# Input weights split once, kept in device memory as two parts, and read back by the later blocks

## The chip, the cores and the metric

The kernel runs on one core of a Trainium2 chip. The metric is device time in microseconds of one execution. A core has TensorE (PE, with its weight loads as PEld), VectorE (DVE), ScalarE (ACT), GpSimd (POOL) and SyncE (SP), each working through a queue of its own in order, and 16 DMA engines, to which here nearly every transfer is issued from SP's queue.

## The reference

One encoder layer over two sequences, of 1024 and 2048 tokens with 1024 features, in float32. A normed residual goes through one input projection. Its columns feed an FNet group (zf, uf) and a bidirectional Mamba-2 group (z, x, B, C, dt), and the two outputs go through an output projection and a gated embedding.

```python
u = rms_norm(h, norm_w)
proj = u @ w_in                     # 1024 -> 2*512 + 1536 + 2560 + 48
z_f, u_f, z_s, xbc, dt_raw = jnp.split(proj, [...], axis=-1)
y_f = einsum(real(fft2(u_f)), w_fmix) * silu(z_f)
xbc = silu(conv1d(xbc, width 5) + conv_b)
xs, Bm, Cm = jnp.split(xbc, [D_SSM, D_SSM + N_BC_GROUPS * D_STATE], axis=-1)
dt_f, dt_b = softplus(dt_raw + bias)
y_s = ssd(xs, dt_f, A_f, Bm, Cm) + flip(ssd(flip(xs), flip(dt_b), ...)) + D * xs
y_s = group_rms_norm(y_s * silu(z_s)) * ssd_norm_w
h = h + concat([y_f, y_s]) @ w_out
h = h + (p @ w_ple_in) * sigmoid(h @ w_ple_gate)
return rms_norm(h, final_norm_w)
```

## The kernel before, in words

The work has two phases. The first, to about 1970 us, is the input projection with the convolution and the state-space scan. It goes over three blocks of 1024 tokens: the short sequence, and the two halves of the long one (with two tokens of overlap). The second phase is the Fourier transform, the output projection and the gated embedding; nothing in it is edited.

In a block, the normed tokens stand transposed in SBUF in three parts of 342 columns, each as a high part uh, rounded to the type in which TensorE reads it, and a low part ul, the remainder. A block has 40 jobs, one per 128 columns of w_in (4 C, 4 B, 12 x, 12 z, 4 uf, 4 zf), and one short job dt. A job's weights are treated as the tokens are: a load brings 128 columns of w_in into wr (512 KB in pieces of 512 bytes), ACT casts it to wh, and POOL subtracts to get wl. wr has one buffer, wh and wl two each. A job has three pieces, one per token part: 24 matmuls into a PSUM bank (wh with uh, wh with ul, wl with uh, for each of eight row groups), and one eviction by ACT. All three blocks load and split the same weights.

The order of all of this is written by hand, in slots. Each piece of a job is a slot; `pre(s, f)` puts f ahead of the piece of slot s in the queues of the engines that it uses, `post(s, f)` behind it. A list `rows_` sets the order of the jobs: the first row interleaves C, dt and B piece by piece, then come uf0 and, for each of 12 units (two heads of the scan), x, z and one other job; the last row interleaves uf3 and zf3. Nine slots make a unit's cycle. A unit's `plan` places its steps by slot: loads of the broadcast rows R (rows_in, 256 KB a piece) and er (decays), POOL's cut of R (rows_cut), ACT's exponentials, DVE's joins, PE's diag, POOL's weighting xw (weighted) for PE's states, the products across, POOL's gating of y with z (in the second block with two more multiplications, L662 and L663) and the stores of y.

`split_at` and `load` of a job are set by the loop over `coming`: a job is split in the slot after the last piece of the job two before it, three slots ahead of its own first piece, and its load is issued one slot behind the split of the job before, which is five slots ahead. The load then waits, on SP, until POOL has read wr for that job.

At a block's start the dt job's result is transposed (dt_turned), goes through a long chain on DVE (dt_softplus, to atm), and is summed by PE (dt_sums, tile pcs, copied by ACT to acs) and transposed again (dt_rows, tile prw), stored, and read back as R and er. In a block's last row, x_in loads the next block's token tiles, x_norm scales them on DVE and x_turn transposes them on PE (tile pt) into uh and ul.

Of the kernel before, what the change touches and what calls it, by code (L numbers as in the profile page):

```python
# [56 lines left out]
def tile_hybrid_encoder(ctx: ExitStack, tc: tile.TileContext, a):  # L57
# [20 lines left out]
    WSd = [dram.tile([P, 7, 4, 512], F32, name=f"WSd{i}") for i in range(3)]  # L78
    PLd = dram.tile([P, 2, DM], F32, name="PLd")
# [22 lines left out]
    with ExitStack() as ph:  # L102
# [76 lines left out]
        def weights_in(c0):  # L179

            raw = wp.tile([P, KT, P], F32, tag="wr", bufs=1, name="wr")
            nc.sync.dma_start(raw, w_in[:, c0:c0 + P].rearrange("(k p) c -> p k c", p=P))
            return raw

        def weights_split(raw):

            wh = wp.tile([P, KT, P], F32R, tag="wh", name="wh")
            wl = wp.tile([P, KT, P], F32R, tag="wl", name="wl")
            S.copy(wh, raw)  # L189
            G.tensor_tensor(wl, raw, wh.bitcast(F32), op=ALU.subtract)  # L190
            return wh, wl

# [43 lines left out]
        U = {}  # L236

# [74 lines left out]
        class Job:  # L312
# [8 lines left out]
            def load(self):  # L321
                self.raw = weights_in(self.c0)

            def split(self):
                self.w = weights_split(self.raw)
# [404 lines left out]
        for bi, B in enumerate(blocks):  # L730
# [3 lines left out]
            rows_.append((B, [J("dt"), J("C"), J("B")] if bi else [J("C"), J("dt"), J("B")], "first"))  # L734
# [10 lines left out]

        n_, coming = 0, []
        for _, js, _ in rows_:
            for k, j in enumerate(js):
                j.last = n_ + 2 * len(js) + k
                if j.c0 is not None:  # L750
                    coming.append(j)
            n_ += 3 * len(js)
        coming[0].split_at = coming[1].split_at = -1
# [21 lines left out]
        with tc.manual_schedule():  # L775
# [23 lines left out]
            for i in range(3, 9):  # L799
                if i > 3:  # L800
                    pre(i - 4, x_norm, b0, i)
                if i > 5:
                    pre(i - 6, x_in, b0, i)
                post(i - 3, x_turn, b0, i)
            pre(9, decay_rates)
            for B, js, what in rows_:
# [24 lines left out]
                for si in range(3):  # L831
                    for j in js:
                        step(lambda: j.piece(si))
# [552 lines left out]
```

## Time and profile before

| | us |
|---|---|
| median of 3 runs | 3038.52 (3036.92 to 3041.12) |
| the profiled execution, whole | 3031.59 |
| its span, first to last instruction | 3029.8 |
| PE busy | 2836.0 (94%) |
| DVE / POOL / ACT busy | 2228.9 / 1475.5 / 1389.1 |
| DMA: share of the 16 engines on SP's queue | 60.6%, 436.50 MB |
| mean granted TensorE clock | 0.972 |

Busy times overlap; only what PE waits for, or what slows its clock, can change the span. Lines are those of the kernel before; an arrow to the left stands between the tile written and those read, or between an instruction and what ended its wait.

### The profile page before, as it was taken

The page shows a single profiled execution, that of the slowest core. Times are in us where ns is not written, and L with a number is a line of the kernel's source. Part 1 is how long each engine was busy: PE and PEld are TensorE (multiplying, and loading weights), DVE is VectorE, ACT ScalarE, POOL GpSimd, SP SyncE. Part 2 cuts the span into 40 slices and gives each one's busy share as a digit, 9 for nine tenths or more (in the row PEclk, how much of TensorE's full clock was granted, in tenths as well). Part 3 has the DMA queues.
Part 4 walks back from the last instruction along what each step waited for, and adds up shares of the span by engine and source line. Part 5 has one row for each costly group of instructions (what it writes and reads, how often), then busy time and mean ns, then how long its engine had stood idle before and what let it go on. Part 6 is the DMA issues. An engine that isn't in the chain of part 4 may idle for free. (4 is left out here: it accounts for less than half of the span.)

```text
span 3029.8 us, 47051 instructions
## 1 busy us (share of the span) xinstructions
PE 2836.0 (94%) x17252; PEld 2566.2 (85%) x17252; DVE 2228.9 (74%) x3412; ACT 1389.1 (46%) x2980; POOL 1475.5 (49%) x1114
## 2 busy tenths in 40 slices
PE   6899999989999899989999999969999899989998
PEld 6899989988999889989999999957677677768887
DVE  3687767666687568666779787687989988875665
ACT  4444545434544454434544444434433533354554
POOL 1355645431567565642555655455777578610000
PEclk9999999999999999999999999979999999999999
DMA  3378878972588778862677787566554644352221
GB/s 96 76 129 162 158 157 173 139 142 79 125 171 167 152 181 165 154 167 64 127 154 146 159 144 158 117 210 250 173 184 132 236 149 150 133 198 91 94 85 69
DMA packets 454579, 440.56 MB, mean 145 GB/s; under 512 B 24384, under 2 KB 405444, under 8 KB 450508
## 3 DMA queue, kind: packets, MB, share of 16 engines
q1 hardware_dynamic: 454060, 436.50, 60.6%
q8 instruction: 137, 2.24, 0.3%
q14 instruction: 94, 0.77, 0.1%
q10 hardware_dynamic: 288, 1.05, 0.1%
HBM read 328.41 MB, written 110.10 MB: 145 GB/s over the span
## 5 line engine op out<-in xcount | busy, mean ns | idle before, releaser
L361 PE MATMUL ps<-uh,wh 128*128 128x342 f32 (+1 forms) x2880 | 961.6, 334 | 8.4 <-ACT uh L267 8.4
L361 PE MATMUL ps<-ul,wh 128*128 128x342 f32 (+1 forms) x2880 | 926.3, 322 | 2.5 <-DVE ul L268 2.5
L361 PE MATMUL ps<-uh,wl 128*128 128x342 f32 (+1 forms) x2880 | 927.4, 322 | 0.4 <-POOL wl L190 0.4
L190 POOL TENSOR_TENSOR wl<-wr,wh 128x1024 fp32r<-128x1024 f32 x120 | 305.5, 2546 | 707.9 <-ACT wh L189 650.5
L361 PEld LDWEIGHTS ps<-uh,wh 128*128 128x128 f32 x2880 | 552.2, 192 | 20.1 <-ACT uh L267 9.2
L361 PEld LDWEIGHTS ps<-ul,wh 128*128 128x128 f32 x2880 | 554.5, 193 | 4.2 <-DVE ul L268 3.5
L361 PEld LDWEIGHTS ps<-uh,wl 128*128 128x128 f32 x2880 | 550.4, 191 | 1.2 <-POOL wl L190 1.1
L558 ACT ACTIVATE R<-R,lb 128x128 f32<-128x128 f32 x1152 | 356.8, 391 | 98.3 <-POOL R L548 98.2
L548 POOL TENSOR_SCALAR_AFFINE_SELECT R<-R 128x512 f32<-128x512 f32 x288 | 257.5, 905 | 193.7 <-DMA R<-ROWd 187.2
L618 DVE SCALAR_TENSOR_TENSOR H<-H,cd,pst 128x64 f32<-128x64 f32 x888 | 182.6, 274 | 47.7 <-PE pst L607 44.6
L402 DVE SCALAR_TENSOR_TENSOR xT<-raw,cvt,xT 128x1024 f32<-128x1024 f32 x144 | 214.8, 1492 | 2.6
L1102 PE MATMUL X<-whP,ah 128*128 128x512 f32 x480 | 195.2, 407 | 8.0 <-ACT pu L1111 6.4
L1102 PE MATMUL X<-wlP,ah 128*128 128x512 f32 x480 | 193.6, 403 | 1.6 <-DVE wlP L861 1.6
L1102 PE MATMUL X<-whP,al 128*128 128x512 f32 x480 | 192.5, 401 | 2.4 <-DVE al L1073 2.4
L587 POOL TENSOR_TENSOR xw<-xm,wd 128x512 f32<-128x512 f32 x144 | 181.8, 1268 | 18.7 <-PE pst L607 18.5
L367 ACT COPY raw<-ps 128x342 f32<-128x342 f32 x180 | 78.3, 438 | 241.7 <-PE ps L361 226.8
L1214 POOL TENSOR_TENSOR ht<-ht,pu 128x512 f32<-128x512 f32 x96 | 151.9, 1590 | 63.1 <-ACT pu L1111 43.0
L607 PE MATMUL pst<-xw,Bm 128*128 128x128 f32 x1056 | 151.3, 285 | 24.0 <-POOL xw L587 23.8
L607 PEld LDWEIGHTS pst<-xw,Bm 128*128 128x128 f32 x1056 | 131.9, 192 | 41.6 <-POOL xw L587 30.3
L189 ACT CAST wh<-wr 128x1024 fp32r<-128x1024 f32 x120 | 125.8, 1049 | 67.9 <-DMA wr<-in_w_in 67.2
L1073 DVE TENSOR_TENSOR al<-s,ah 128x512 fp32r<-128x512 f32 x144 | 143.6, 1021 | 16.4 <-ACT ah L1072 16.3
L563 DVE TENSOR_TENSOR R<-R,R 128x512 f32<-128x512 f32 x144 | 134.1, 931 | 25.9 <-ACT R L558 23.5
(264 smaller groups left out, 5703.9 us busy)
## 6 DMA issues: line engine op xcount, KB each, us to landing
R<-ROWd SPq DMA_DIRECT2D x288, 256.0 KB
wr<-in_w_in SPq DMA_DIRECT2D x120, 512.0 KB
er<-EXPd SPq DMA_DIRECT2D x288, 128.0 KB
Hd<-ht SPq DMA_DIRECT2D x48, 512.0 KB
ht<-Hd SPq DMA_DIRECT2D x48, 512.0 KB
y<-Yd SPq DMA_DIRECT2D x46, 512.0 KB
wlP<-WSd SPq DMA_DIRECT2D x21, 1024.0 KB
Yd<-y SPq DMA_DIRECT2D x72, 256.0 KB
```

The lines of the kernel that those rows point to most:

```text
L190: G.tensor_tensor(wl, raw, wh.bitcast(F32), op=ALU.subtract)
L361: T.matmul(ps[:, :n], lhsT=wt[:, kt, :], rhs=ut[:, kt, :n], start=(i == 0), stop=(i == 3 * KT - 1))
L402: V.scalar_tensor_tensor(dst, raw[:, k:k + TB], cvt[:, 20 * k + ct:20 * k + ct + 1], dst, op0=ALU.mult, op1=ALU.add)
L548: G.affine_select(out=R.rearrange("p c h l -> p (c h) l"), in_=R.rearrange("p c h l -> p (c h) l"), pattern=[[0, 4], [sgn, P]], compare_op ...
L558: S.activation(R[:, c, h, :], R[:, c, h, :], AF.Exp, bias=self.B.lb[:, 2 * p + c, hc + h:hc + h + 1])
L563: V.tensor_tensor(E[0], E[0], E[1], op=ALU.add)
L587: G.tensor_tensor(xw, self.xm[c4].rearrange("p c (h e) -> p c h e", h=2), col(self.B.wd[:, c4:c4 + 4, hc:hc + 2]).broadcast_to([P, 4, 2, 6 ...
L607: T.matmul(pst[:, c, :], lhsT=B.Bm[self.g][:, c4 + c, :], rhs=xw[:, c, :, :].rearrange("p h e -> p (h e)"), start=True, stop=True)
L618: V.scalar_tensor_tensor(dst[:, e], H[d][:, cc, e], B.cd[:, cc, hc + h:hc + h + 1], pst[:, c, e], op0=ALU.mult, op1=ALU.add)
L1073: V.tensor_tensor(al, src, ah.bitcast(F32), op=ALU.subtract)
L1102: T.matmul(ps, lhsT=at[:, k, :], rhs=wt[:, k, :], start=(first and i == 0), stop=(i == 11), skip_group_check=not first)
L1214: return lambda t: G.tensor_tensor(h, h, t, op=ALU.add)
```

## The change

The first block splits each job's weights as before, and two slots behind the split it stores wh and wl to device memory (WPd, 512 KB each, in rows of 4 KB). The second and third blocks load both parts into wh and wl and round them in place with two ACT copies; they have no subtraction on POOL. In all blocks a job's load now stands in the slot after the last piece of the job two before (three slots ahead of its first piece), and the split or rounding one slot ahead of the first piece. B has a row of its own behind the first one; the last row's pieces take another order; the steps of dt and of the next block's tokens have other slots.

```diff
+    WPd = [[dram.tile([P, KT, P], F32, name=f"WPd{i}_{x}") for x in range(2)] for i in range(C_DT // P)]
...
             def load(self):
-                self.raw = weights_in(self.c0)
+                if self.B.bi == 0:
+                    self.raw = wp.tile([P, KT, P], F32, tag="wr", bufs=1, name="wr")
+                    nc.sync.dma_start(self.raw, w_in[:, self.c0:self.c0 + P].rearrange("(k p) c -> p k c", p=P))
+                else:
+                    self.w = self.places()
+                    for x, wt in enumerate(self.w):
+                        nc.sync.dma_start(flat(wt).bitcast(F32), flat(WPd[self.c0 // P][x]))
+
+            def places(self):
+                return [wp.tile([P, KT, P], F32R, tag=f"w{x}", name=f"w{x}") for x in "hl"]
 
             def split(self):
-                self.w = weights_split(self.raw)
+                if self.B.bi == 0:
+                    self.w = wh, wl = self.places()
+                    S.copy(wh, self.raw)
+                    G.tensor_tensor(wl, self.raw, wh.bitcast(F32), op=ALU.subtract)
+                    for x, wt in enumerate(self.w):
+                        pre(slot[0] + 2, nc.sync.dma_start, flat(WPd[self.c0 // P][x]), flat(wt).bitcast(F32))
+                else:
+                    for wt in self.w:
+                        S.copy(flat(wt), flat(wt).bitcast(F32))
...
-                    conv(16 + i, self.dst, CT, s_ + (2 if i else 4))
+                    conv(16 + i, self.dst, CT, s_ + (2 if i else 3))
...
-            rows_.append((B, [J("dt"), J("C"), J("B")] if bi else [J("C"), J("dt"), J("B")], "first"))
+            rows_.append((B, [J("dt"), J("C")] if bi else [J("C"), J("dt")], "first"))
+            rows_.append((B, [J("B")], None))
...
+                turn = [(0, 0), (0, 1), (1, 0), (0, 2), (1, 1), (1, 2)]
...
-            j, k = coming[m], coming[m - 1]
-            j.split_at = max(coming[m - 2].last + 1, k.split_at + 2)
-            pre(k.split_at + 1, j.load)
-            pre(j.split_at, j.split)
+            j = coming[m]
+            j.load_at = coming[m - 2].last + 1
+            pre(j.load_at, j.load)
+            pre(max(j.first - 1, j.load_at), j.split)
...
-            for i in range(3, 9):
+            for i, (n_in, n_norm, n_turn) in enumerate(
+                    ((0, 0, 0), (0, 0, 0), (0, 0, 1), (0, 1, 2), (1, 2, 2), (1, 2, 3)), 3):
...
-                    post(q + 7, dt_turned, B)
-                    pre(q + 8, dt_softplus, B, 0)
-                    pre(q + 9, dt_softplus, B, 1)
-                    post(s0 + 13, dt_sums, B)
-                    post(s0 + 14, dt_rows, B)
-                    pre(s0 + 16, dt_out, B)
+                    post(q + 5, dt_turned, B)
+                    pre(q + 6, dt_softplus, B, 0)
+                    pre(q + 7, dt_softplus, B, 1)
+                    post(q + 10, dt_sums, B)
+                    post(q + 12, dt_rows, B)
+                    pre(q + 14, dt_out, B)
...
-                    for i, s_ in enumerate((2, 3, 4, 4, 5, 6, 8, 9, 10)):
-                        pre(s0 + (0, 0, 1, 2, 2, 3, 5, 6, 7)[i], x_in, b, i)
+                    for i, s_ in enumerate((3, 4, 5, 5, 6, 7, 7, 8, 9)):
+                        pre(s0 + (0, 0, 1, 2, 3, 4, 5, 6, 7)[i], x_in, b, i)
```

What this moves is seen best in three queues. The first is SP's in the middle of the first block, through some five slots of a unit's cycle: wr is a weight load, er and R are the broadcast rows, Yd and WPd stores. Before:

```order
L182 DMA wr<-in_w_in 128x8x128
L667 DMA Yd_60<-y 128x512
L540 DMA R_3261<-ROWd_67 128x2x256
L540 DMA R_3263<-ROWd_67 128x2x256
L635 DMA er_3318<-EXPd_70 64x4x128 x2
L635 DMA er_3321<-EXPd_70 64x4x128 x2
L182 DMA wr<-in_w_in 128x8x128
L635 DMA er_3434<-EXPd_70 64x4x128 x2
L635 DMA er_3437<-EXPd_70 64x4x128 x2
```

And with the change:

```order
L315 DMA wr<-in_w_in 128x8x128
L192 DMA wb<-in_w_out 128x2x256 x2
L676 DMA Yd_60<-y 128x512
L549 DMA R_3371<-ROWd_67 128x2x256
L549 DMA R_3373<-ROWd_67 128x2x256
L278 DMA WPd_0_130<-wh 128x1024
L278 DMA WPd_1_131<-wl 128x1024
L644 DMA er_3434<-EXPd_70 64x4x128 x2
L644 DMA er_3437<-EXPd_70 64x4x128 x2
L315 DMA wr<-in_w_in 128x8x128
```

Two stores per job now stand ahead of the er loads and of the next weight load, which holds its place behind the first four er loads.

The second is the same queue at the same place of the third block. Before:

```order
L182 DMA wr<-in_w_in 128x8x128
L667 DMA Yd_62<-y 128x512
L540 DMA R_17481<-ROWd_69 128x2x256
L540 DMA R_17483<-ROWd_69 128x2x256
L288 DMA UFd_64<-ft 128x1024
L635 DMA er_17544<-EXPd_72 64x4x128 x2
L635 DMA er_17547<-EXPd_72 64x4x128 x2
L182 DMA wr<-in_w_in 128x8x128
```

With the change:

```order
L319 DMA wh<-WPd_0_108 128x1024
L319 DMA wl<-WPd_1_109 128x1024
L192 DMA wb<-in_w_ple_gate 128x2x256 x2
L676 DMA Yd_62<-y 128x512
L549 DMA R_17637<-ROWd_69 128x2x256
L549 DMA R_17639<-ROWd_69 128x2x256
L278 DMA UFd_64<-ft 128x1024
L644 DMA er_17702<-EXPd_72 64x4x128 x2
L644 DMA er_17705<-EXPd_72 64x4x128 x2
L319 DMA wh<-WPd_0_158 128x1024
L319 DMA wl<-WPd_1_159 128x1024
```

Each weight load has become two, at the same point between the other transfers, but for a job that is due two slots sooner; and where it waited for POOL's reading of wr it now waits for PE's last piece of the job two before.

The third is ACT's at the start of the second block, around the copy of the sums, acs (ft and raw are evictions of pieces, CT and BT the convolutions' tiles, rows the transposed sums). Before:

```order
L406 ACTIVATE CT<-raw,cvt 128x1024
L406 ACTIVATE BT<-raw,cvt 128x1024
L371 COPY ft<-ps 128x342
L371 COPY ft<-ps 128x340
L189 CAST wh<-wr 128x1024
L367 COPY raw<-ps 128x342
L410 ACTIVATE raw<-CT 128x1024
L410 ACTIVATE raw<-BT 128x1024
L367 COPY raw<-ps 128x342
L471 COPY acs<-pcs 128x512
```

With the change:

```order
L334 CAST wh<-wh 128x1024
L334 CAST wl<-wl 128x1024
L376 COPY raw<-ps 128x342
L380 COPY ft<-ps 128x342
L419 ACTIVATE raw<-CT 128x1024
L415 ACTIVATE BT<-raw,cvt 128x1024
L380 COPY ft<-ps 128x342
L480 COPY acs<-pcs 128x512
```

The copy of the sums stood behind the tanh of both C and B, and now stands behind that of C alone.

More of the change, by code (lines that the diff above doesn't have):

```diff
@@ L177, in dt_weights @@
             V.tensor_tensor(wdt[:, :, 1, :], wdr, wdt[:, :, 0, :].bitcast(F32), op=ALU.subtract)
[L179 to L191, printed above, removed]
         def weight_sums(i, s0):
@@ L236, in tile_hybrid_encoder, with flat @@
         U = {}
+        def flat(t):
+            return t.rearrange("p k c -> p (k c)")
         def x_normed(b, i, xn):
@@ L743, in tile_hybrid_encoder @@
             rows_.append((B, [J("uf", 3), J("zf", 3)], "last"))
-        n_, coming = 0, []
[L747 to L753, printed above, removed]
+        pieces = []
+        for B, js, what in rows_:
+            if what == "last":
+                turn = [(0, 0), (0, 1), (1, 0), (0, 2), (1, 1), (1, 2)]
+            else:
+                turn = [(k, si) for si in range(3) for k in range(len(js))]
+            pieces.append([(js[k], si) for k, si in turn])
+        n_, coming = 0, []
+        for row in pieces:
+            for j, si in row:
+                if si == 0:
+                    j.first = n_
+                    if j.c0 is not None:
+                        coming.append(j)
+                j.last = n_
+                n_ += 1
         for m in range(2, len(coming)):
-            j, k = coming[m], coming[m - 1]
-            j.split_at = max(coming[m - 2].last + 1, k.split_at + 2)
-            pre(k.split_at + 1, j.load)
-            pre(j.split_at, j.split)
+            j = coming[m]
+            j.load_at = coming[m - 2].last + 1
+            pre(j.load_at, j.load)
+            pre(max(j.first - 1, j.load_at), j.split)
         xs = {}
@@ L830, in tile_hybrid_encoder @@
                             pre(s0 + 2 * i, norm_piece, BLOCKS[bi + 1], i)
-                for si in range(3):
-                    for j in js:
-                        step(lambda: j.piece(si))
+                for j, si in row:
+                    step(lambda: j.piece(si))
             while before or behind_:
```

12 lines of the change are left out of this document (6 added, 6 removed).

## The prediction

> **What bounds the kernel now.** I read the profile by stretches first: the three blocks' long middle parts (from a block's first z job to the start of its last row of jobs) and the two borders between them. The columns are microseconds, then busy time of each engine with its count, the granted TensorE clock, the share of the 16 DMA engines, and GB/s.
>
> ```profile
> 107.90:631.50 523.60, 511.70 (x3580) 493.16 (x3579) 375.26 (x649) 264.21 (x604) 276.61 (x218) 0.99 0.80 147
> 631.50:751.30 119.80, 105.41 (x695) 100.46 (x694) 81.72 (x116) 42.39 (x90) 32.52 (x22) 0.93 0.48 110
> 751.30:1300.50 549.20, 519.87 (x3603) 499.16 (x3601) 389.53 (x669) 266.24 (x605) 332.08 (x258) 0.98 0.77 157
> 1300.50:1420.00 119.50, 105.75 (x697) 100.69 (x696) 81.83 (x118) 42.47 (x90) 44.32 (x30) 0.93 0.44 119
> 1420.00:1937.60 517.60, 512.91 (x3624) 495.12 (x3622) 395.16 (x674) 246.10 (x570) 275.43 (x218) 1.00 0.71 143
> ```
>
> The three middle parts do nearly the same matmuls (3580 to 3624). The third block has PE busy 512.9 of 517.6 us at full clock: nothing can be won there. The first is 6 us longer, the second 31.6 us longer. The two borders run at clock 0.93 with 14 us of idle PE each. So PE bounds the kernel, and the change, which leaves every matmul in place, can only win what these stretches lose: some 32 us in the second block, the borders, and the start.
>
> The waits of PE (and then of the split) say what the second block loses. The first two rows are the second block's middle part alone: total wait, number, longest. The last two are groups of the page: busy time and mean ns, then idle time before and what ended it.
>
> ```profile
> PE pst L607 <- POOL xw L587: 17.4, 11, 3.8
> PE pd L575 <- ACT wh L189: 6.2, 1, 6.2
> ...
> L190 POOL TENSOR_TENSOR wl<-wr,wh 128x1024 fp32r<-128x1024 f32 x120 | 305.5, 2546 | 707.9 <-ACT wh L189 650.5
> L189 ACT CAST wh<-wr 128x1024 fp32r<-128x1024 f32 x120 | 125.8, 1049 | 67.9 <-DMA wr<-in_w_in 67.2
> ```
>
> POOL makes the low part wl in 2.55 us, 120 times, and its queue stands 650.5 us behind ACT's cast for it. The weighted inputs xw, for which PE waits, are next in that queue.
>
> **The change, part by part.** *POOL and ACT in blocks two and three.* 80 subtractions of 2.55 us (204 us) leave POOL; ACT gets 80 more copies of 1.05 us (84 us). ACT is busy 246 of 517.6 us in the third block, so 42 us more there lie beside PE; only their lateness can cost (below). In the second block the xw waits (17.4 us, plus half clock behind the longer ones) lose their cause in the queue. POOL keeps three multiplications per half unit there, and the pd wait (6.2 us) stems from ACT standing before a load, which the change keeps. I take 20 of the 31.6 us; bounds 0 (POOL late by its own work) and 32.
>
> *The dt chain.* It moves two pieces earlier, and between sums and rows stand two pieces instead of one. Start, duration, instruction; in brackets the idle time and its releaser:
>
> ```profile
> 716.76 0.86 DVE L433 TENSOR_TENSOR pv<-ptd,pv 128x256 f32<-128x256 f32 x2 [8.78 <-ACT pv L432]
> 726.27 4.23 DVE L461 SCALAR_TENSOR_TENSOR dtm<-dtm,dz 128x512 f32<-128x512 f32 x3
> 730.54 2.87 DVE L441 SCALAR_TENSOR_TENSOR dtm<-dtm,dz 128x512 f32<-128x512 f32 x4
> 733.44 0.69 DVE L442 SCALAR_TENSOR_TENSOR dtm<-dtm,de 128x512 f32<-128x512 f32 x1
> 734.17 2.77 DVE L443 SCALAR_TENSOR_TENSOR dtm<-dtm,dmx 128x512 f32<-128x512 f32 x1
> 736.98 0.69 DVE L446 TENSOR_TENSOR atm<-dtm,arep 128x512 f32<-128x512 f32 x1
> 737.59 2.60 DVE L402 SCALAR_TENSOR_TENSOR CT<-raw,cvt,CT 128x1024 f32<-128x1024 f32 x2
> ...
> 725.93 2.57 POOL L190 TENSOR_TENSOR wl<-wr,wh 128x1024 fp32r<-128x1024 f32 x1 [5.29 <-ACT wh L189]
> 733.56 2.83 POOL L190 TENSOR_TENSOR wl<-wr,wh 128x1024 fp32r<-128x1024 f32 x1 [5.06 <-ACT wh L189]
> ...
> 724.46 0.45 ACT L371 COPY ft<-ps 128x342 f32<-128x342 f32 x1 [3.47 <-PE ps L361]
> 731.98 0.44 ACT L371 COPY ft<-ps 128x340 f32<-128x340 f32 x1 [3.31 <-PE ps L361]
> 745.31 1.06 ACT L410 ACTIVATE raw<-CT 128x1024 f32<-128x1024 f32 x1 [9.14 <-DVE CT L402]
> 749.12 0.59 ACT L471 COPY acs<-pcs 128x512 f32<-128x512 f32 x1
> ...
> 749.76 1.91 PE L493 MATMUL prw<-ident,acs 128*64 128x128 f32 x8 [4.81 <-ACT acs L471]
> ```
>
> ACT stood 9.1 us before the C tanh, acs came behind it, and PE waited 4.81 us. Now: the DVE chain from pv (716.8) to atm (737.7) takes 20.9 us, of which L461 and L443 lose about 2.1 us each (three at 0.72 are 2.15, not 4.23; 0.69, not 2.77) exactly while POOL runs wl. Without wl it is 16.7 us. Two evictions 7.52 us apart two pieces on give 3.76 us a piece, so the sums stand five pieces (18.8 us) behind the turned dt, and the rows seven (26.3 us). Only the C taps (two of 2.60) then lie ahead of acs, with tanh and the small copies some 8.5 us: 25.2 us, just in time. In the first block wl stays; I leave 3 us there. The wait and its half clock:
>
> ```profile
> 745.00:750.00 5.00, 0.24 (x2) 0.21 (x3) 4.93 (x6) 3.23 (x5) 0.00 (x0) 0.84 0.00 0
> 750.00:755.00 5.00, 5.00 (x21) 4.76 (x20) 2.56 (x5) 4.21 (x7) 0.00 (x0) 0.50 0.01 2
> ...
> PE prw L493 <- ACT acs L471: 17.2, 3, 7.6
> ```
>
> At clocks 0.84 and 0.50 the two stretches lose 3.3 us beside the wait. Three waits of 17.2 us and 9.9 us of clock are 27.1; I take -24 (bounds -27 and -10, if DVE is as late as now).
>
> *The borders.* Each first x tile gets one more piece between its load and its transposes, the last three one less. PE's waits for these transposes, first border and then second:
>
> ```profile
> PE pt L264 <- DVE H L618: 5.0, 2, 3.5
> PE pt L264 <- DVE xt L250: 4.4, 1, 4.4
> ...
> PE pt L264 <- DVE H L618: 6.3, 2, 3.3
> PE pt L264 <- DVE xt L250: 2.2, 1, 2.2
> ```
>
> These are 17.9 us; clock 0.93 over 119.8 us loses 8.4 a border, less the 3.3 of acs, so 10.2 for both: 28 in all. One piece is about the longest wait (4.4), but the three late tiles have less room: -18 (bounds -28 and 0).
>
> *The start.* The second and third parts of the first block are wanted one and two pieces earlier. PE already waits there:
>
> ```profile
> PE ps L361 <- ACT uh L267: 8.4, 3, 6.4
> ```
>
> A piece less of cover is about 4 us; some of it comes back at its loads, which are also earlier: +5 (bounds 0 and +12).
>
> *The stores.* In the first block SP issues two stores of 512 KB per job behind the row loads, and the loads R, er and wr queue behind their bytes. The trace has no such store; the price comes from a late stretch whose DMAs are 512 KB pieces:
>
> ```profile
> 2850.00:2925.00 75.00, 75.00 (x355) 61.16 (x354) 50.36 (x81) 41.93 (x81) 0.00 (x0) 1.00 0.23 81
> ...
> 160.00:175.00 15.00, 15.00 (x108) 14.61 (x107) 14.00 (x22) 6.23 (x14) 7.04 (x4) 1.00 1.00 119
> 190.00:205.00 15.00, 15.00 (x108) 14.24 (x107) 14.86 (x27) 8.72 (x22) 8.28 (x7) 1.00 0.59 106
> ```
>
> 0.23 of 75 us moved 6.1 MB, so 1.05 MB take 3.0 us of all engines. A job lasts 15.2 us (517.6 us for the 34 jobs of the third middle part), so 34.4 jobs add 103 us to 0.80 of 523.6 us (419): 522, a share of 1.00. Stretches of 15 us do reach 1.00 while PE runs without a gap, others have 0.59, so the room is there, but all of it is used. If it fits, the cost is 0; if the engines hold no more than 0.90 over the block, the part lasts 580 us, +56. I take +25, nearer to fitting since PE bore 1.00 for single stretches. In blocks two and three the loads double, at 0.77 and 0.71 of the engines, so the share stays below the first block's.
>
> *Weights later.* Until now loads were issued five pieces before use and split three before; now the load stands three pieces ahead, the rounding one. In the later blocks it also waits until PE has done with the buffers, so it has 15.2 us. Issue and cast behind it, second block and third:
>
> ```profile
> 893.28 0.38 SPq L182 DMA_DIRECT2D wr<-in_w_in  x1
> 907.01 1.05 ACT L189 CAST wh<-wr 128x1024 fp32r<-128x1024 f32 x1 [4.56 <-DMA wr<-in_w_in]
> ...
> 1602.37 0.38 SPq L182 DMA_DIRECT2D wr<-in_w_in  x1
> 1613.27 1.05 ACT L189 CAST wh<-wr 128x1024 fp32r<-128x1024 f32 x1
> ...
> 1153.56 0.66 PE L575 MATMUL pd<-R,xm 128*64 128x128 f32 x8 [2.48 <-ACT R L558]
> 1154.00:1158.00 4.00, 4.00 (x20) 3.85 (x16) 3.96 (x10) 1.58 (x6) 0.00 (x0) 0.58 0.90 193
> ```
>
> At most 10.9 us to land in the third block; with half of the 3.0 us for the second part and two casts of 1.05 that is 14.5 of 15.2: just in time. In the second 13.7 + 3.6 is 17.3: 2.1 us late, for the one load in three that follows the er loads, some 11 times: 23 us there, and half clock behind the longer ones, as behind the 2.48 us wait (clock 0.58 in the next 4 us). ACT, blocked in front of these casts, delays evictions and R's exponentials too. POOL's relief lets SP run earlier: +10 (bounds 0 and +45).
>
> By the Trainium skill (TensorE: Matmul & The Clock Gate, § Why this matters for your kernels) only idle gaps over about 3 us drop the clock, so late weights of 2 us would cost no clock. This trace shows half clock after 2.48 us, so it does not bear the rule out at that length. By the rule this term would be some 5 us lower, and the sum with it.
>
> Sum: -20 - 24 - 18 + 5 + 25 + 10 = -22 against the profiled execution's 3031.6 us (span 3029.8): 3009.6. The median of the runs, 3038.5, is 6.9 above it: 3016.
>
> **The rivals.** *B, the stores fill the DMA queue: slower.* The place is the first block's middle part, the price above. Without the stores the sum is -47, so it decides above +53, where the DMA engines stay under 522/577 = 0.90. At 0.90 the time is 3048, at 0.85 (614 us, +90) 3081. For it: 1.00 needed on average where 0.80 was held, and one queue on which the loads PE depends on follow the stores. Against it: PE loses little today with 1.00 in single stretches.
>
> *C, all cover holds.* Stores and weights cost nothing, the second block becomes the third (-32), borders and acs go whole (-28, -27), start +4: -83, 2956. For it: DVE, too, gains 2.1 us wherever wl stood beside an operation as at 726 and 734, up to 80 times in blocks two and three. Against it: the loads' 13.7 us. The Trainium skill (SBUF — State Buffer, § Who interferes with whom) has DVE instructions with two SBUF inputs block on GpSimd ones that read SBUF; the two rows agree.
>
> *D, no change.* PE takes the same waits under other names: xw's become those for R's loads or for wh, and the stores eat the borders. 3038. For it: waits of PE in block two end on ACT behind a load as well.
>
> **How the numbers follow.** The forecast A has 0.44 (2995 to 3032), B 0.28, C 0.12, D 0.16. A measurement of this kernel tells 0.2%, 6 us, from no change. Faster holds A and C, 0.56; same D, 0.16; slower B, 0.28. The range cuts the outer third or so of B and most of C: 2975 to 3072.
>
> **What would show it.** Right: no PE wait for acs in blocks two and three, second middle part near 530 us, xw waits under 5 us, wl's group at 40 in POOL, first middle part near 550 us with a DMA share over 0.95. Wrong: PE waits ending on casts of wh and wl, repeated each third job; a first part over 575 us; x-tile waits still at the borders; half clock spread through blocks two and three.

## The result, and the profile after

The changed kernel takes 3134.94 us (median; 3133.49 to 3143.27) where the kernel before takes 3038.43 on the same chip: ratio 1.0322 (95% interval 1.0303 to 1.0342), 96.5 us slower. The forecast was 3016 us, faster, in a range of 2975 to 3072. The profiled execution took 3133.49 us with a span of 3131.7.

The same stretches as before the change (first middle part, border, second, border, third), in the profile after; columns as in the prediction:

```profile
107.60:676.70 569.10, 526.34 (x3580) 502.26 (x3579) 358.14 (x645) 260.69 (x596) 263.03 (x219) 0.97 0.82 197
676.70:814.20 137.50, 112.49 (x696) 105.55 (x695) 79.56 (x132) 52.90 (x102) 20.91 (x18) 0.88 0.53 142
814.20:1372.90 558.70, 524.29 (x3602) 502.31 (x3601) 340.69 (x653) 291.60 (x628) 227.34 (x224) 0.97 0.79 185
1372.90:1501.10 128.20, 108.04 (x698) 101.66 (x697) 76.18 (x122) 55.20 (x105) 25.41 (x24) 0.89 0.50 140
1501.10:2037.00 535.90, 518.36 (x3625) 497.61 (x3623) 340.26 (x669) 272.26 (x594) 166.63 (x184) 0.99 0.72 172
```

The stretches are longer by 45.5, 17.7, 9.5, 8.7 and 18.3 us; the start is the same, and what follows 2037 is 2.5 us longer. The same matmuls keep PE busy for 14.6 us more in the first part: its granted clock fell from 0.99 to 0.97. The other 31 us are idle time.

PE's waits in the three middle parts, two rows for each:

```profile
PE ps L370 <- POOL wl L329: 25.8, 15, 2.9
PE ps L370 <- ACT wh L328: 16.1, 8, 5.9
...
PE ps L370 <- ACT wh L334: 22.8, 8, 6.0
PE ps L370 <- ACT wl L334: 10.7, 10, 1.9
...
PE ps L370 <- ACT wh L334: 10.7, 7, 3.0
PE ps L370 <- ACT wl L334: 6.6, 8, 1.4
```

But for 1.5 us, PE waits there for weights alone. No wait for xw is left (17.4 us in the second part before), and none for acs. POOL's group of subtractions has shrunk as foreseen, and POOL now stands idle behind the loads of R for 603.8 us, where it was 187.2:

```profile
L329 POOL TENSOR_TENSOR wl<-wr,wh 128x1024 fp32r<-128x1024 f32 x40 | 99.8, 2494 | 338.7 <-ACT wh L328 294.2
L334 ACT CAST wh<-wh 128x1024 fp32r<-128x1024 f32 x80 | 84.1, 1051 | 112.4 <-DMA wh<-WPd 112.4
L557 POOL TENSOR_SCALAR_AFFINE_SELECT R<-R 128x512 f32<-128x512 f32 x288 | 220.9, 772 | 809.8 <-DMA R<-ROWd 603.8
```

One of these waits in the first block, from the timeline: the load, the er loads behind it, the cast, PE's first matmul of the job, and its third, the first that reads wl.

```profile
298.70 3.41 SPq L315 DMA_DIRECT2D wr<-in_w_in  x1
302.73 9.32 SPq L644 DMA_DIRECT2D er<-EXPd  x4
314.00 1.04 ACT L328 CAST wh<-wr 128x1024 fp32r<-128x1024 f32 x1 [6.60 <-DMA wr<-in_w_in]
315.09 0.42 PE L370 MATMUL ps<-uh,wh 128*128 128x342 f32 x1 [2.84 <-ACT wh L328]
317.54 0.65 PE L370 MATMUL ps<-uh,wl 128*128 128x342 f32 x1 [1.87 <-POOL wl L329]
```

And the clock (the third number from the end) in the 4 us behind it:

```profile
318.00:322.00 4.00, 4.00 (x20) 4.00 (x20) 2.40 (x6) 0.00 (x0) 1.52 (x3) 0.69 0.94 263
```

The load is issued at 298.70 and cast at 314.00, 15.3 us later. PE would have started 2.84 us earlier. Two matmuls on it stands another 1.87 us, until POOL has made wl from the same cast, and behind the two waits its clock falls to 0.69. By the rule of the Trainium skill that the prediction weighed (TensorE: Matmul & The Clock Gate, § Why this matters for your kernels) gaps of under about 3 us cost no clock. With two waits so close, this row cannot test it; the prediction's row at 1153.56, a wait of 2.48 us with no other near it, speaks against it. Most of the long waits come once per unit, at the same one of its nine slots, whose load is issued between the two groups of er loads.

### The profile page after: what moved, and what is told of

Same layout as the page of the kernel before. It is cut to its first block, busy times and chain, and to the rows that moved or that the text cites. A ratio compares the mean times of both kernels' runs of the same rounds, so it can differ in the third digit from the quotient of the medians.

```text
span 3131.7 us, 47440 instructions
## 1 busy us (share of the span) xinstructions
PE 2871.1 (92%) x17252; PEld 2589.3 (83%) x17252; DVE 2096.8 (67%) x3412; ACT 1467.5 (47%) x3060; POOL 1218.5 (39%) x1034
## 5 line engine op out<-in xcount | busy, mean ns | idle before, releaser
L370 PE MATMUL ps<-uh,wl 128*128 128x342 f32 (+1 forms) x2880 | 943.1, 327 | 50.4 <-POOL wl L329 30.9
L370 PEld LDWEIGHTS ps<-uh,wl 128*128 128x128 f32 x2880 | 558.2, 194 | 64.8 <-POOL wl L329 37.4
L557 POOL TENSOR_SCALAR_AFFINE_SELECT R<-R 128x512 f32<-128x512 f32 x288 | 220.9, 772 | 809.8 <-DMA R<-ROWd 603.8
L329 POOL TENSOR_TENSOR wl<-wr,wh 128x1024 fp32r<-128x1024 f32 x40 | 99.8, 2494 | 338.7 <-ACT wh L328 294.2
L596 POOL TENSOR_TENSOR xw<-xm,wd 128x512 f32<-128x512 f32 x144 | 169.2, 1177 | 104.1 <-PE pst L616 85.9
L411 DVE SCALAR_TENSOR_TENSOR xT<-raw,cvt,xT 128x1024 f32<-128x1024 f32 x144 | 194.9, 1354 | 2.6
L263 DVE SCALAR_TENSOR_TENSOR zT<-zT,ps 128x342 f32<-128x342 f32 (+1 forms) x108 | 54.8, 507 | 171.7 <-ACT zT L262 171.1
L661 DVE TENSOR_TENSOR yt<-po,er 128x512 f32<-128x512 f32 (+1 forms) x144 | 91.3, 634 | 110.0 <-PE po L658 86.7
```

What stands on the lines that cost most here:

```text
L329: G.tensor_tensor(wl, self.raw, wh.bitcast(F32), op=ALU.subtract)
L370: T.matmul(ps[:, :n], lhsT=wt[:, kt, :], rhs=ut[:, kt, :n], start=(i == 0), stop=(i == 3 * KT - 1))
L411: V.scalar_tensor_tensor(dst, raw[:, k:k + TB], cvt[:, 20 * k + ct:20 * k + ct + 1], dst, op0=ALU.mult, op1=ALU.add)
L557: G.affine_select(out=R.rearrange("p c h l -> p (c h) l"), in_=R.rearrange("p c h l -> p (c h) l"), pattern=[[0, 4], [sgn, P]], compare_op ...
L596: G.tensor_tensor(xw, self.xm[c4].rearrange("p c (h e) -> p c h e", h=2), col(self.B.wd[:, c4:c4 + 4, hc:hc + 2]).broadcast_to([P, 4, 2, 6 ...
L661: V.tensor_tensor(t[:, cr], po[:, cr], self.er[d, c4][:, cr], op=ALU.mult)
```

## The experiments

Chips differ by about 1%. The kernel before took 3038 us on the one of the changed kernel, 3020 on that of the two runs with earlier er loads, and 3052 to 3056 on those of all other runs, so times of different chips are compared by their ratios alone. A stretch comes from one execution, which can lie 0.4% off the median (the moved steps alone: 3056.5 against 3043.4, so that their stretches are long ones). In us, from rows like those above:

| | ratio | first part | border | second | border | third |
|---|---|---|---|---|---|---|
| kernel before (3038) | 1 | 523.6 | 119.8 | 549.2 | 119.5 | 517.6 |
| changed kernel (before at 3038) | 1.0322 | 569.1 | 137.5 | 558.7 | 128.2 | 535.9 |
| moved steps alone | 0.9967 | 526.8 | 120.7 | 557.6 | 121.8 | 520.7 |
| and late loads | 1.0048 | 525.1 | 130.8 | 547.3 | 131.5 | 521.2 |
| and both parts read, no stores | 1.0096 | 528.4 | 126.4 | 564.1 | 129.3 | 530.8 |
| changed, block one's loads early | 1.0360 | 577.7 | 138.4 | 566.0 | 130.6 | 542.3 |
| early loads, all blocks store both parts | 1.0543 | 586.2 | 130.0 | 596.0 | 124.5 | 564.5 |
| the same, one part | 1.0173 | 542.3 | 121.4 | 574.4 | 124.1 | 536.4 |
| the same, half of both parts | 1.0209 | 543.6 | 122.3 | 574.8 | 121.3 | 535.7 |
| one part, in pieces of 512 bytes | 1.0380 | 561.5 | 125.9 | 593.8 | 125.6 | 540.7 |
| changed, stores from ACT | 1.0304 | 579.9 | 133.0 | 558.0 | 127.8 | 533.2 |
| changed, weight sums out of block one | 1.0287 | 557.1 | 136.3 | 575.3 | 134.0 | 540.1 |
| changed, er loads earlier (before at 3020) | 1.0271 | 567.5 | 136.4 | 549.1 | 125.9 | 521.1 |

**The change taken apart.** Four kernels.

Moved steps alone: nothing of the weights is changed (the code below with all three blocks in the first branch, `load` and `split` as for the first block, no stores).

```diff
+            if j.B.bi in (0, 1, 2):
+                j.split_at = max(coming[m - 2].last + 1, k.split_at + 2)
+                pre(k.split_at + 1, j.load)
+            else:
+                j.load_at = coming[m - 2].last + 1
+                j.split_at = max(j.first - 1, j.load_at)
+                pre(j.load_at, j.load)
```

> The changed order of jobs, dt steps and token tiles (B in a row of its own, the last row's turn, the slots of dt, x_in, x_norm, x_turn) is kept; the weights are handled as in the kernel before: all blocks load wr five slots ahead and split it three ahead, no WPd stores or loads. Theory L (the loss is the weights' load standing two slots later): the prediction's terms for dt, borders and start are left, -24 - 18 + 5 = -37 to the kernel before, 3001 us; middle parts as before (524, 549, 518). Theory S (the loss is the added bytes: stores in block one, double loads in blocks two and three): the same 3001. Theory R (the moved steps themselves cost): the borders keep the +17.7 and +8.7 us that the changed kernel shows there, so about 3065.

Measured: 0.9967 (0.9948 to 0.9985), 10 us faster and not 37. The waits for acs are gone.

Late loads alone: the same with `in ()`.

> As the kernel with the moved steps alone, but every load of wr stands three slots ahead of its job's first piece and the split one slot ahead, in all three blocks; no stores, no second part, so no byte more than before. Theory L: PE waits for casts and wl once per unit in every block; first middle part about 560 us (569 in the changed kernel less the stores' few us), second and third as much longer than before, 30 to 40 us each, since wl still takes 2.5 us of POOL there: 3100 to 3130. Theory S: about 3001, no weight waits over 5 us per middle part. Theory R: about 3065.

Measured: 1.0048 (1.0029 to 1.0067), 25 us above the moved steps, where theory L wanted 100. In the profiled executions the middle parts are no longer than with early loads; the two borders are, by 10 us each. As wholes these two executions are only 7 us apart (3063.3 and 3056.5), so where the rest of the 25 us lies is not shown. In the first part 14.1 us of weight waits are left:

```profile
106.40:631.50 525.10, 510.99 (x3581) 490.72 (x3579) 365.17 (x644) 262.02 (x595) 271.91 (x219) 0.99 0.78 147
```

The load of the same job as the one at 298.70 above, in this run's timeline:

```profile
282.79 0.38 SPq L315 DMA_DIRECT2D wr<-in_w_in  x1
295.94 1.05 ACT L328 CAST wh<-wr 128x1024 fp32r<-128x1024 f32 x1 [2.45 <-DMA wr<-in_w_in]
298.85 0.40 PE L368 MATMUL ps<-uh,wh 128*128 128x342 f32 x1
```

Here it takes 13.2 us to its cast, and is issued 16.1 us before PE wants it; with the stores it took 15.3, and was issued 13.6 us before. Over the whole first part a load's way from issue to cast is little longer with the stores (median 12.3 us, 11.1 without), but SP spends 361 us on issuing where it spent 284, only 49 of these on the stores themselves; the other 28 us more go to the transfers around them.

Block one early in the changed kernel: `in (0,)`, stores kept.

> The changed kernel with one edit: in block one the load of wr stands five slots ahead and the split three ahead, as in the kernel before; stores stay, blocks two and three load both parts three slots ahead. Theory L: the first middle part falls from 569 to 525-535 us, the rest stays: about 3095. Theory S: the first middle part keeps most of its 45 us over the kernel before, 555 or more: 3120 to 3135.

Measured: 1.0360 (1.0341 to 1.0379), the first part 577.7. Theory L falls: with the stores in the queue, more lead does not help at all. PE then waits no longer for weights in the first part, but 31.2 us for xw, which POOL makes behind wl.

Stores in all blocks, early loads, nothing reads them:

> The kernel with the moved steps alone, plus the stores of wh and wl in all three blocks (each job of each block stores its two parts; nothing reads them): wr five slots ahead in all blocks. 120 jobs times 1.05 MB of stores more than the kernel with the moved steps alone. Theory L: the stores fit beside PE; at most 10 us a block, 3001 to 3030. Theory S: 45 us in the first middle part and as much in the other two, about 3130. Theory R: 3065 and no more than 10 us a block above it.

Measured: 1.0543 (1.0513 to 1.0574). By the profiled executions the stores cost 59, 38 and 44 us in the three middle parts, in the third too, whose DMA share was 0.70:

```profile
108.80:695.00 586.20, 525.21 (x3580) 505.61 (x3579) 374.54 (x647) 262.06 (x601) 265.00 (x218) 0.96 0.85 193
825.00:1421.00 596.00, 534.55 (x3601) 513.58 (x3601) 390.07 (x670) 261.55 (x597) 314.42 (x258) 0.95 0.83 206
1545.50:2110.00 564.50, 528.49 (x3623) 509.55 (x3622) 395.10 (x675) 243.47 (x564) 270.35 (x218) 0.96 0.81 196
```

**How the stores cost.** One part stored, instead of two:

```diff
-                    for x, wt in enumerate(self.w):
+                    for x, wt in [(0, wh)]:
```

> The kernel with the moved steps and early loads, storing one part (wh) of every job in all three blocks instead of two: half the bytes of the run that stored both, which stood at 1.0543 against 0.9967 without stores, 175 us for 240 stores. Theory P (each store costs the same, 0.73 us): 88 us, ratio 1.025. Theory T (a threshold: stores are free until a unit's cycle has no idle DMA time left): well under half, 15 to 40 us, ratio 1.002 to 1.010.

Measured: 1.0173 (1.0149 to 1.0198), 63 us for half the stores where all cost 175: between the two theories, and more than in proportion for the second half. ACT's idle time before its casts, in the group of the page, shows where it begins. Without stores:

```profile
L328 ACT CAST wh<-wr 128x1024 fp32r<-128x1024 f32 x120 | 125.8, 1049 | 104.4 <-DMA wr<-in_w_in 104.3
```

With one part stored:

```profile
L328 ACT CAST wh<-wr 128x1024 fp32r<-128x1024 f32 x120 | 125.9, 1049 | 191.0 <-DMA wr<-in_w_in 187.2 <-DMA er<-EXPd 3.6
```

With both:

```profile
L328 ACT CAST wh<-wr 128x1024 fp32r<-128x1024 f32 x120 | 125.8, 1048 | 295.1 <-DMA wr<-in_w_in 290.1 <-DMA R<-ROWd 4.9
```

The wait for wr goes from 104 to 187 to 290 us. With early loads PE meets it not as a wait for weights but for xw, behind a late wl in POOL's queue: 41.3 us in the whole run without stores, 53.5 with one part stored, 122.1 with both.

As many stores, each of half the columns (`[:, :512]` on both sides):

> As the run that stored both parts of every job in all blocks with early loads (ratio 1.0543), but each store takes only half of the columns: 240 stores of 256 KB in rows of 2 KB. As many stores for SP to issue, half the bytes. Theory Y (what costs is the bytes' time on the DMA engines): as with one whole store per job, ratio 1.012 to 1.022. Theory I (what costs is the issue on SP's queue, 0.7 to 1.1 us a store, ahead of the loads): as with two whole stores, 1.045 to 1.055.

Measured: 1.0209 (1.0177 to 1.0240): as half the bytes, not as all the stores. What SP spends on issuing them is not what costs: in the first part that is 76 us, where the stores of one whole part took 34, and the two first parts are as long (543.6 and 542.3).

One part stored, in pieces of 512 bytes (`WPd` as KT x P x P):

> As the run that stored one part (wh) of every job in all blocks with early loads (ratio 1.0173), but WPd is laid out so that the store goes in pieces of 512 bytes and not of 4 KB: same bytes, same number of stores, eight times the pieces. Theory Y in bytes alone: 1.017 again. Theory G (the DMA engines' time, which goes by pieces too, is what is short): clearly more, 1.03 to 1.06, with R and wr waited for longer.

Measured: 1.0380 (1.0356 to 1.0405). Against the moved steps alone, the same bytes in the same number of stores cost twice as much (0.041 for 0.021). SP took no longer to issue them (36 us in the first part, 34 in rows of 4 KB), but 61 us where it took 26 for the weight loads behind them. So the pieces count beside the bytes, as theory G had it. That the engines' time goes by pieces is not borne out: by the DMA packets of the two traces, the stores took much the same time of all 16 engines in the first part, 49 us in pieces of 512 bytes and 43 in rows of 4 KB.

The stores from ACT's queue:

```diff
-                        pre(slot[0] + 2, nc.sync.dma_start, flat(WPd[self.c0 // P][x]), flat(wt).bitcast(F32))
+                        pre(slot[0] + 2, nc.scalar.dma_start, flat(WPd[self.c0 // P][x]), flat(wt).bitcast(F32))
```

> The changed kernel with one edit: the stores of wh and wl are issued from ACT's queue and not from SP's, so that they go into a DMA queue of their own and no load of R, er or wr stands behind them in order; bytes, slots and timing are the same. Theory Q (the loads lose their place in the one queue to the stores): the first middle part falls from 569 us to 540 or less, the whole to 3090-3105 where the kernel before takes 3038 (ratio 1.017 to 1.022). Theory E (the stores take time of the DMA engines, whichever queue they come from): the first middle part stays at 560 or more, the ratio at 1.03 or more.

Measured: 1.0304 (1.0277 to 1.0332), as the changed kernel. It does not settle it alone, since the stores now also stood before evictions on ACT; but the loads came no sooner: in the first part PE's waits for weights rose from 41.9 to 53.8 us, and POOL's for R from 52.0 to 79.3. The Trainium skill (DMA: Bandwidth & Descriptors, § Issuing engines are not separate DMA queues) says that transfers started by several engines run on the same 16 DMA engines and interleave; this run agrees, as the stores cost the same from either queue (1.0304 and 1.0322).

Room in block one: its weight sums (loads of wb, stores of WSd) are made in the other two.

```diff
-                    if 2 <= what < 10:
-                        weight_sums(8 * bi + what - 2, s0)
+                    if bi:
+                        weight_sums(12 * (bi - 1) + what, s0)
```

> The changed kernel with one edit: the sums of the output weights (wb loads of 512 KB and WSd stores of 896 KB per unit, in eight units of each block) are left out of block one and made in all twelve units of blocks two and three, 11 MB less in block one where the stores of WPd are some 36 MB in its middle part. The WPd stores stand where they stood in the order. Theory G (what is short in block one is the time of the DMA engines as a whole): the first middle part falls from 569 us to about 550, by the runs with no, half and all stores (526, 542, 570 to 586); ratio 1.022 to 1.030, since blocks two and three take some of it back. Theory O (what costs is the place of the two stores, right ahead of the loads of er and wr): 563 or more, ratio 1.030 or above.

Measured: 1.0287 (1.0267 to 1.0307), the first part 557.1 at a share of 0.80: 12 of some 45 us come back (15 with the chips' 0.6% taken off), and the other blocks are longer. The sums' own work has left block one too (POOL is busy 237.6 us in the first part where it was 263.0), so the run does not show the traffic alone. The part gets shorter, but a mean share of 0.80, as before the change, does not free PE of the waits (33.2 us for weights are left of 41.9).

**What the loads cost.** The changed kernel without the stores; blocks two and three read the two parts of one job again and again, so the output is not the layer's:

```diff
-                    for x, wt in enumerate(self.w):
+                    for x, wt in enumerate(self.w if self.kind == "uf" and self.i == 0 else ()):
...
-                        nc.sync.dma_start(flat(wt).bitcast(F32), flat(WPd[self.c0 // P][x]))
+                        nc.sync.dma_start(flat(wt).bitcast(F32), flat(WPd[C_UF // P][x]))
```

> The changed kernel without the stores of the first block, but for those of uf0: all jobs of blocks two and three bring the two parts of that one job (their weights are wrong, their bytes, rows and timing those of the changed kernel). So the double loads alone are left beside the moved steps and the later loads. Theory SB (stores cost block one, the double loads the other two): first middle part 525 us as with late loads alone, second and third near the changed kernel's 559 and 536; ratio about 1.017. Theory SO (the stores alone cost, what is lost in blocks two and three comes from the later loads): second and third at 545 and 520, ratio about 1.005, as with late loads alone.

Measured: 1.0096 (1.0075 to 1.0117), between the theories; the first part is back at 528.4. The second parts (wl beside wh) cost 15 us (1.0096 less 1.0048), what POOL's relief brings taken in. Whether reading other memory each time would cost more or less, this run cannot tell. The stores of block one are then worth 1.0322 less 1.0096, 69 us: some 44 in the first part and 12 at the first border, with the chips' 0.6% taken off.

The er loads, two slots earlier and so behind the weight load of that slot:

```diff
-                    pre(s0 + 11, self.decays, d, 0)
+                    pre(s0 + 9, self.decays, d, 0)
```

> The changed kernel with one edit: the first four er loads of a unit are issued two slots earlier, behind the weight load of that slot, so that the weight load which the pieces wait for once per unit no longer stands right behind them; all bytes and the stores stay. Theory O (the place: one load per unit stands behind the er loads): PE's waits for weights, 113.6 us in the changed kernel, fall below 60, the middle parts from 569, 559 and 536 to about 545, 545 and 525; ratio 1.012 to 1.020. Theory G (the queue is behind as a whole, another load of the cycle is late instead): waits over 90, ratio 1.027 or more.

Measured: 1.0271 (1.0247 to 1.0295), at the edge of theory G as a whole, with 86.1 us of PE's waits for weights, between the two theories; but the blocks differ. The chip is 0.6% faster than the changed kernel's.

```profile
106.70:674.20 567.50, 523.15 (x3581) 498.55 (x3579) 358.06 (x646) 262.23 (x596) 265.00 (x219) 0.97 0.85 197
810.60:1359.70 549.10, 522.02 (x3602) 502.19 (x3600) 336.74 (x655) 293.91 (x630) 222.45 (x226) 0.97 0.83 190
1485.60:2006.70 521.10, 514.21 (x3624) 494.96 (x3622) 336.12 (x667) 273.87 (x594) 169.88 (x184) 1.00 0.78 176
```

PE's waits for weights in the second and third of these stretches:

```profile
PE ps L370 <- ACT wh L334: 11.8, 4, 4.8
PE ps L370 <- ACT wl L334: 8.1, 8, 1.9
...
PE ps L370 <- ACT wl L334: 3.2, 5, 1.2
PE ps L370 <- ACT wh L334: 1.7, 2, 1.1
```

In the third block weight waits fell from 17.3 to 4.9 us: there the place of one load behind the er loads is most of what cost. In the second they fell from 33.5 to 19.9, by less than half. In the first block, where the stores are, nothing came back.

**The moved steps, and a faster version.** B back in the first row and dt's steps in their old slots, with the moved token steps left:

> Only the last row's turn, the next block's token slots and the start's are as in the changed kernel; B stands again in the first row, dt's steps in the slots of the kernel before, wr in all blocks, early loads, no stores. With dt's steps moved too the ratio was 0.9967. If the dt move brought that gain (its three waits for acs, 17 us before, are gone there): 0.999 to 1.002 here, with PE's waits for acs back. If the token move brought it: 0.995 to 0.997 here, borders without their waits for x tiles.

Measured: 1.0022 (1.0007 to 1.0037). With dt's steps moved too it was 0.9967, so the dt move, with B's row of its own, is worth 0.55%, 17 us, and the token move, with the start's, costs some 7. The first border of this run:

```profile
PE pt L254 <- DVE H L625: 7.3, 2, 4.2
PE prw L500 <- ACT acs L478: 4.8, 1, 4.8
PE pst L614 <- POOL xw L594: 4.0, 1, 4.0
```

The transposes no longer wait for a late xt, but longer for DVE's H (5.0 us before); the wait for acs is back, 17.2 us in three as before the change.

Loads four slots ahead and splits two, without stores:

> The kernel with the moved steps alone (no stores, wr in all blocks), with the load four slots and the split two slots ahead of the first piece in the long middle parts, five and three elsewhere. The run with loads at three slots and splits at one had a second middle part 10 us shorter than the one with five and three, and borders 10 us longer each. Theory A (ACT, standing before a load at its cast, holds up R's exponentials and so xw: a split later than three ahead frees it): second middle part 545-550 us and borders as with early loads; ratio 0.990 to 0.994. Theory N (the two runs differ by chance): 0.997, as with the moved steps alone.

Measured: 0.9979 (0.9964 to 0.9994), theory N; the second part stayed at 556.6.

Two multiplications of the second block's gating on DVE, with the moved steps:

```diff
-                    G.tensor_tensor(er_b, er_b, col(elt[:, c4:c4 + 4, self.u]).broadcast_to([P, 4, P]), op=ALU.mult)
-                    G.tensor_tensor(zT[:, tk], er_b.rearrange("p c l -> p (c l)"), zT[:, tk], op=ALU.mult)
+                    V.tensor_tensor(er_b, er_b, col(elt[:, c4:c4 + 4, self.u]).broadcast_to([P, 4, P]), op=ALU.mult)
+                    V.tensor_tensor(zT[:, tk], er_b.rearrange("p c l -> p (c l)"), zT[:, tk], op=ALU.mult)
```

> The kernel with the moved steps alone (no stores, wr in all blocks, early loads; 0.9967), and in the second block the two multiplications of the gating that only that block has (er by elt, then by zT; 48 instructions, 64.7 us of POOL) run on DVE. Theory A (POOL's own work there makes xw late, 26 us of PE's waits in the second middle part): that part falls from 557 to 530-545 us, xw waits there under 10 us; ratio 0.988 to 0.993. Theory N (what makes xw late is R and wr landing late): no gain, 0.995 to 1.000.

Measured: 0.9962 (0.9948 to 0.9976). In the profiled execution the second part was 542.0 us with 2.0 us of xw waits, as theory A had it, but as a whole it can't be told from the moved steps alone. It is, with those, the best that was found: some 11 us faster than the kernel before.

Both of the last two together:

> No stores, wr in all blocks, the moved steps, loads four and splits two slots ahead in the middle parts (0.9979 alone), and the second block's two extra gating multiplications on DVE (0.9962 alone, second middle part 542 us where the steps alone had 557). If the two add up: second middle part 530 to 540 us, ratio 0.990 to 0.994. If both take away the same waits for xw: 0.995 to 0.997.

Measured: 0.9964 (0.9949 to 0.9979): the gains do not add. And with the er loads earlier as well:

> As the run without stores with loads four and splits two slots ahead and the two extra gating multiplications on DVE (0.9964), with the first four er loads of a unit two slots earlier as well. If a part of what is left there (casts and R late behind er) goes: 0.990 to 0.994. If not: 0.995 to 0.998.

Measured: 1.0153 (1.0128 to 1.0178). With wr in all blocks the earlier er loads do harm (first part 543.8, ACT's wait for wr 176.8 us where it was 119.2); what helped the changed kernel is no rule.

## Why the prediction was wrong

Term by term, in us of 3038:

| term | forecast | measured | from |
|---|---|---|---|
| dt chain | -24 | -17 | 0.9967 less 1.0022 |
| borders and start | -13 | +7 | 1.0022 |
| weights later (wr alone) | +10 | +25 | 1.0048 less 0.9967 |
| second parts, with POOL's relief | -20 | +15 | 1.0096 less 1.0048 |
| stores in block one | +25 | +69 | 1.0322 less 1.0096 |
| sum | -22 | +99 | 96.5 in the whole |

Each row is the difference of two ratios, and these form a chain from the kernel before to the changed one, so that the sum comes out near the whole of itself and says nothing about the single rows.

*The stores.* This is the step that failed most: "I take +25, nearer to fitting since PE bore 1.00 for single stretches". A stretch of 15 us at full share says that the engines can be full while PE has its data; it does not say that a whole block can be. The part ended at a share of 0.82, far from the 1.00 that the sum wanted, and yet the stores cost it some 44 us. Their own price was not far off: packets of 4 KB took 104 us of all engines there, 18 before the change, so 85 more where the sum had 103. What failed is adding them to a fixed 419 us. The packets of 1 KB, most of them R's, took 202 us instead of 248, and all together 464: a share below 1.00 says neither that a transfer fits nor that it costs nothing. Rival B had the outcome (the queue falls behind) and, with 0.85, nearly the share. That the loads follow the stores in one queue is not needed for it, since from ACT's queue the stores cost as much. Its point of decision was wrong, since half the stores already cost 15 us in the first part, and the third block lost 44 us to stores where 0.81 was reached. A mean below 0.90 proved to be no room: a unit's loads come in bunches, and the load behind the er loads had, as the 298.70 row shows, under 14 us for a way of 15.

*Weights later.* The mechanism was right, down to the one job in three, and the prediction named these waits among its signs of being wrong. The size was not right: +10 was taken, less than the 23 us worked out for the second block, because POOL's relief would let SP run earlier. That block lost 27.5 us in these waits with wr alone and 33.5 in the changed kernel, and the third 17.3 there. The first block was not priced for it at all; by the profiled executions late loads alone cost nothing there in the middle part, and 10 us at the border behind it, which the term had not looked at.

*Second block.* The waits for xw went (17.4 to 0) and the weights' waits took their place: rival D's exchange, at a higher price. The doubled loads had been given 1.5 us of a load's way and no further cost, because the share stayed below the first block's (it did, at 0.79 and 0.72); with the relief taken in they cost 15 us. What the relief alone is worth was not shown.

*dt chain.* Right within its bounds (-27 and -10): no wait for acs is left in any block.

*Borders and start.* Wrong. With the chips' 0.5% taken off, the run with the token move alone has a start 1.9 us longer, a first border 2.3 longer and a second 0.5 shorter, so the 18 us at the borders were not won; the rest of the +7 is not at the borders, and one execution does not show where it comes from. The late xt was one of two causes at the border; the other, DVE's H ahead of the tokens' own work in its queue, stayed, and the tiles are now wanted sooner. In the changed kernel weights are late there as well.

*The signs.* Of the right ones, no wait for acs, xw under 5 us and wl's group at 40 came true; the lengths did not (558.7 us for 530 in the second part, 569.1 for 550 in the first), nor did a share over 0.95. Of the wrong ones, casts of wh and wl repeated each third job, waits for tokens at the borders, and clocks of 0.97 and 0.99 came true; a first part over 575 us did not.

Open: which limit of the DMA engines makes the queue fall behind at a share of 0.8 was not found. The traces give one place to look, which no run tested: in the first part before the change the packets of 1 KB hold 248 of the 419 us, with a mean of 117 ns but a median of 46, so that a part of the share is slow packets and not bytes. Stores shifted past the weight load were not tried: they would have had to land before the next cast into the same buffer.

## What to carry to other kernels

Price an added transfer by the lead that the loads around it have left, and by its pieces as well as its bytes, not by the mean share of the DMA engines; one run that adds the transfer alone tells it. Before moving work off one engine, ask whether the loads that feed the rest have any lead left: here a load with 15 us on its way had 14. And take the parts of a change apart on the chip: one of five was worth its 17 us, and the other four hid it.

## What the runs showed of the hardware

The share of the DMA engines is no measure of what they can still take: stores in pieces of 512 bytes cost twice as much as the same bytes in 4 KB rows, at a share of 0.78 for 0.83 in the first part. The first part with one part stored in rows of 4 KB:

```profile
105.50:647.80 542.30, 517.94 (x3579) 498.92 (x3579) 370.89 (x647) 264.47 (x602) 273.77 (x218) 0.97 0.83 177
```

And in pieces of 512 bytes:

```profile
106.90:668.40 561.50, 523.09 (x3581) 503.85 (x3579) 374.99 (x647) 263.55 (x602) 265.93 (x218) 0.96 0.78 171
```

Likewise 1 MB read in two parts of 4 KB rows took no more of the engines than 0.5 MB read in 512-byte pieces: the second part ran at a share of 0.76 and 184 GB/s with the two parts, and at 0.78 and 157 GB/s with wr and the same late loads.

Half clock follows PE waits of under 3 us as well, but not always. Over the 18 traces, take the waits with no other over 0.5 us in the 5 us before or the 4 us behind them: half clock set in within 4 us behind 152 of the 253 of 1.7 to 2.9 us, and behind 98 of the 99 of 3.3 to 6.1 us.
